# A hybrid state-space and delta-rule layer: the delta rule's inverse and decays on GpSimd, and two scalings of the state space as one GpSimd instruction for four heads

## The chip, the cores and the metric

The kernel runs on one core of a Trainium2 chip. The metric is the device time of one execution in microseconds (us), the median of several runs. The engines are TensorE (PE, with PEld for its weight loads), VectorE (DVE), ScalarE (ACT), GpSimd (POOL) and SyncE (SP), which issues nearly all DMAs. Each engine works through its own list of instructions in order; the lists meet only through semaphores.

## The reference

One layer over 1024 latent tokens and 256 context tokens of width 2048. The input is normed and modulated, multiplied by w_in, and the product is split; a short convolution follows, then two mixers side by side, a norm, and the product with w_out. The two places of the change lie in the mixers:

```
# delta rule (gdn_scan): 8 heads, 2 directions, chunks of 128 tokens
decay = exp(where(incl, gcum[:, None] - gcum[None, :], -inf))
a_strict = where(strict, (k_beta @ k.T) * decay, 0)
sol = triangular_solve(a_strict, rhs, unit_diagonal=True)
S = S * dec + ke.T @ v_new                  # scan over 10 chunks

# state space (ssd_scan): 16 heads in quarters of 4, 2 directions
lmat = exp(where(causal, seg, -inf))        # seg: differences of cumulated decays
states = B.T @ (x * dt * decay_end)
h = h * dec + states                        # scan over 10 chunks
```

## The kernel before, in words

The program is written as steps: blocks of 128 columns of the input projection ("g" for the delta rule, "s" for the state space, "z" for the gate), and for each head h of the delta rule "P" (prep), "I" (invert), "C" (chain) and "E" (end). A static scheduler of the kernel's framework orders the instructions of each engine when the program is built, and puts work of several steps between one another. So, while the chain of head h runs, TensorE also does the prep of head h+1 and products of the next blocks (line 437, 48 matmuls to a group, called *fill* below), and DVE the inverse of head h+1.

**Prep** (gdn_prep) goes over 10 chunks. A tile gb (four buffers) is loaded with the cumulated decays of both directions; `decay` (line 676) subtracts the column's own value and takes the minimum with a causal mask; ACT takes exp (690); DVE multiplies it with TensorE's k-by-k product into A (697), and with the k-by-q product (700), which is stored.

**invert_blocks** follows at once. DVE transposes the 32-wide diagonal blocks of A (715), they go to DRAM and come back as a tile X of 80 partitions, one block in each (721). Then 30 steps, each of two dependent instructions (726, 728), invert all of them: step k works on (31-k) rows of k numbers. X goes to DRAM (730) and comes back as xc (732).

**I** (invert) makes the full inverse from it: DVE transposes xc (741), ACT copies the blocks into A (746, 747), DVE fills the tile et (750 to 753), and TensorE's small products (770 to 794) do the rest. The last of them (794) ends the step. **C** (gdn_chain) is a scan of 10 steps for each of two directions; a step goes TensorE 850 and 852, DVE 856 (r), TensorE 866, DVE 871 and ACT 873 (x), TensorE 876 and 888, DVE 881 (the new state S) and 889 (the output o, from step 2 on). Each step loads its operand vq by an SP DMA (813). `finish_pair` (829 to 835) scales finished outputs, with five short GpSimd instructions to a pair.

**The state space** (ssd_quarter) runs four quarters of four heads. In `state`, ACT scales x by a column for each of four heads (941); GpSimd multiplies the old state (949). For the decays, a tile E is loaded, ACT adds a bias for each head and direction (989, eight instructions to a chunk), DVE selects and ACT takes exp.

In what follows C0 to C7 are the stretches in which the chains of heads 0 to 7 run; each ends with the last product (794) of the next head's I.

Of the kernel before, what the change touches and what calls it, by code (L numbers as in the profile page):

```python
# [14 lines left out]
P = 128  # L15
# [29 lines left out]
class Layer:  # L45
# [627 lines left out]
    def decay(self, e, d, h, c):  # L673

        nc = self.nc
        nc.vector.scalar_tensor_tensor(out=e, in0=e, scalar=self.G[:, 32 + d * 8 + h, c:c + 1],  # L676
                                       in1=self.mneg[:, d], op0=ALU.subtract, op1=ALU.min)

    def gdn_prep(self, h, D):
        nc, sp = self.nc, self.gp  # L680
# [24 lines left out]
    def invert_blocks(self, A):  # L705

        nc, sp = self.nc, self.gp
        t_ = lambda shape, name, **kw: sp.tile(shape, F32, tag=name, name=name, **kw)
        Q = 2 * NCH
        ft = t_([P, NCH, 32], "ft")  # L710
        d1 = self.dram.tile([Q, 4, 32, 32], F32, tag="d1", name="d1", bufs=2)
        d2 = self.dram.tile([Q, 4, 32, 32], F32, tag="d2", name="d2", bufs=2)
        for b in range(4):
            s = slice(32 * b, 32 * b + 32)
            nc.vector.transpose(out=ft[s], in_=A[s, 0, :, s])
            nc.sync.dma_start(out=d1[NCH:, b].rearrange("q j i -> j q i"), in_=A[s, 1, :, s])
        nc.sync.dma_start(out=d1[0:NCH].rearrange("q b j i -> (b j) q i"), in_=ft)

        X = t_([P, NCH * P], "X")[0:4 * Q, 0:1024].rearrange("p (a b) -> p a b", b=32)
        tp = t_([4 * Q, 256], "tp")  # L720
        nc.sync.dma_start(out=X, in_=d1.rearrange("q b j i -> (q b) j i"))
        for k in range(1, 31):
            m = 31 - k
            t = tp[:, 0:m * k].rearrange("p (a b) -> p a b", b=k)
            sh = [4 * Q, m, k]
            nc.vector.tensor_tensor(out=t, in0=X[:, k + 1:, k:k + 1].to_broadcast(sh),  # L726
                                    in1=X[:, k:k + 1, 0:k].to_broadcast(sh), op=ALU.mult)
            nc.vector.tensor_tensor(out=X[:, k + 1:, 0:k], in0=X[:, k + 1:, 0:k], in1=t, op=ALU.add)  # L728
        nc.gpsimd.memset(X.rearrange("p a b -> p (a b)")[:, ::33], 1.0)
        nc.sync.dma_start(out=d2.rearrange("q b j i -> (q b) j i"), in_=X)  # L730
        xc = t_([P, Q, 32], "xc")
        nc.sync.dma_start(out=xc, in_=d2.rearrange("q b j i -> (b j) q i"))
        return xc
# [181 lines left out]
    def ssd_quarter(self, Q, xT, BT, CT):  # L915
        nc, sp = self.nc, self.sp
        t_ = lambda shape, name, **kw: sp.tile(shape, F32, tag=name, name=name, **kw)
        R, PD = 4, 64
        hs = [slice(d * 16 + Q * R, d * 16 + Q * R + R) for d in range(2)]
        bc = lambda ap, n: ap.unsqueeze(2).to_broadcast([P, R, n])  # L920
        if Q % 2 == 0:
            self.btok = t_([P, NCH, P], "btok")
            for g, n in ((0, 4), (4, 4), (8, 2)):
                pt = self.ps("y")
                for i in range(n):
                    self.transpose(pt[:, i * P:(i + 1) * P], BT[:, (g + i) * P:(g + i + 1) * P])
                nc.scalar.copy(out=self.btok[:, g:g + n].rearrange("p c k -> p (c k)"), in_=pt[:, 0:n * P])
        btok = self.btok
        h4 = lambda ap: ap.rearrange("p (r q) -> p r q", q=PD)
        xs = t_([P, NCH, R, PD], "xs", bufs=2)  # L930

        def xtok(c):
            px = self.ps("x")
            for b in range(2):
                self.transpose(px[:, b * P:(b + 1) * P], xT[b][:, c * P:(c + 1) * P])
            nc.scalar.copy(out=xs[:, c], in_=h4(px[:, 0:2 * P]))

        def state(d, c, H, first):
            xd = t_([P, R, PD], "xd", bufs=3)
            for r in range(R):  # L940
                nc.scalar.activation(out=xd[:, r], in_=xs[:, c, r], func=AF.Copy, scale=self.dtw[:, hs[d].start + r, c:c + 1])
            pst = self.ps("h")[:, 0:R * PD]
            nc.tensor.matmul(out=pst, lhsT=btok[:, c], rhs=xd.rearrange("p r q -> p (r q)"),  # L943
                             start=True, stop=True)
            Hn = t_([P, R, PD], f"H{d}", bufs=2)
            if first:
                nc.scalar.copy(out=Hn, in_=h4(pst))
            else:
                nc.gpsimd.tensor_tensor(out=Hn, in0=H, in1=bc(self.cd[:, hs[d], c], PD), op=ALU.mult)
                nc.vector.tensor_tensor(out=Hn, in0=h4(pst), in1=Hn, op=ALU.add)  # L950
            return Hn

        def before(d, c, H):


            y = t_([P, 2, P], f"y{d}", bufs=3)
            for j in range(2):
                nc.sync.dma_start(out=y[64 * j:64 * j + 64],
                                  in_=self.er[hs[d], c * P:(c + 1) * P].rearrange("(b j) t -> j b t", j=2)[j].partition_broadcast(64))
            po = self.ps("z")[:, 0:R * PD]  # L960
            for b in range(2):
                nc.tensor.matmul(out=po[:, b * P:(b + 1) * P], lhsT=H[:, 2 * b:2 * b + 2].rearrange("p r q -> p (r q)"),  # L962
                                 rhs=CT[:, c * P:(c + 1) * P], start=True, stop=True)
            nc.vector.tensor_tensor(out=y, in0=po.rearrange("p (b t) -> p b t", t=P), in1=y, op=ALU.mult)
            return y

        H = None
        for i, c in enumerate([9, 8, 7, 6, 5, 4, 3, 2, 1, 0]):
            xtok(c)
            if c < NLC:  # L970
                y = before(1, c, H)
                for b in range(2):
                    xo = xT[b][:, c * P:(c + 1) * P]
                    nc.vector.scalar_tensor_tensor(out=xo, in0=xo, scalar=self.ssd_d[:, 2 * Q + b:2 * Q + b + 1],  # L974
                                                   in1=y[:, b], op0=ALU.mult, op1=ALU.add)
            if i < NCH - 1:
                H = state(1, c, H, i == 0)
        H = None
        for i, c in enumerate([8, 9, 0, 1, 2, 3, 4, 5, 6, 7]):
            s = slice(c * P, (c + 1) * P)  # L980
            if c < NLC:
                E = t_([P, 2, R, P], "E", bufs=2)
                for d in range(2):
                    nc.sync.dma_start(out=E[:, d], in_=self.gr[hs[d], s].partition_broadcast(P))

                for d in range(2):
                    for r in range(R):
                        j = d * 16 + Q * R + r
                        nc.scalar.activation(out=E[:, d, r], in_=E[:, d, r], func=AF.Identity, bias=self.G[:, j, c:c + 1])  # L989
                nc.vector.copy_predicated(out=E[:, 0], mask=self.mask[:, 1].bitcast(I32).unsqueeze(1).to_broadcast([P, R, P]), data=E[:, 1])  # L990
                nc.scalar.activation(out=E[:, 0], in_=E[:, 0], func=AF.Exp)
                nc.vector.copy_predicated(out=E[:, 0], mask=self.ident.bitcast(I32).unsqueeze(1).to_broadcast([P, R, P]),
                                          data=bc(self.dts[:, Q * R:Q * R + R, c], P))
                pc = self.ps("x")[:, 0:P]
                nc.tensor.matmul(out=pc, lhsT=BT[:, s], rhs=CT[:, s], start=True, stop=True)
                nc.vector.tensor_tensor(out=E[:, 0], in0=E[:, 0], in1=pc.unsqueeze(1).to_broadcast([P, R, P]), op=ALU.mult)
                y = before(0, c, H)
                for b in range(2):
                    nc.gpsimd.tensor_tensor(out=xT[b][:, s], in0=y[:, b], in1=xT[b][:, s], op=ALU.add)
                py = self.ps("y")  # L1000
                for r in range(R):
                    o = r % 2 * PD
                    nc.tensor.matmul(out=py[o:o + PD, r // 2 * P:r // 2 * P + P], lhsT=xs[:, c, r], rhs=E[:, 0, r],  # L1003
                                     start=True, stop=True)
                for b in range(2):
                    nc.vector.tensor_tensor(out=xT[b][:, s], in0=py[:, b * P:(b + 1) * P], in1=xT[b][:, s], op=ALU.add)
            if i < NCH - 1:
                H = state(0, c, H, i == 0)
        for b in range(2 if Q < 2 else 0):
            nc.sync.dma_start(out=self.yr[2 * Q + b], in_=xT[b][:, 0:NL])  # L1010
# [309 lines left out]
```

## Time and profile before

| | us |
|---|---|
| median of 3 runs (lowest, highest) | 2357.67 (2355.03, 2359.08) |
| the profiled execution's own time | 2351.73 |
| its span, first to last instruction | 2350.0 |
| TensorE busy | 2162.5 |
| DVE busy | 1399.5 |
| ACT busy | 998.5 |
| GpSimd busy | 268.7 |

Busy times come from one profiled execution. A TensorE that is shown as busy isn't at its peak: matmuls overlap, and the ends are modelled.

### The profile page before, as it was taken

The page shows a single profiled execution, that of the slowest core. Times are in us where ns is not written, and L with a number is a line of the kernel's source. Part 1 is how long each engine was busy: PE and PEld are TensorE (multiplying, and loading weights), DVE is VectorE, ACT ScalarE, POOL GpSimd, SP SyncE. Part 2 cuts the span into 40 slices and gives each one's busy share as a digit, 9 for nine tenths or more (in the row PEclk, how much of TensorE's full clock was granted, in tenths as well). Part 3 has the DMA queues.
Part 4 walks back from the last instruction along what each step waited for, and adds up shares of the span by engine and source line. Part 5 has one row for each costly group of instructions (what it writes and reads, how often), then busy time and mean ns, then how long its engine had stood idle before and what let it go on. Part 6 is the DMA issues. An engine that isn't in the chain of part 4 may idle for free. (4 is left out here: it accounts for less than half of the span.)

```text
span 2350.0 us, 41855 instructions
## 1 busy us (share of the span) xinstructions
PE 2162.5 (92%) x16070; PEld 1379.2 (59%) x16070; DVE 1399.5 (60%) x3499; ACT 998.5 (42%) x2493; POOL 268.7 (11%) x514
## 2 busy tenths in 40 slices
PE   4989999889999898998989999999999999899998
PEld 4334644456665655556555566555555555788887
DVE  5335543869694856858568486566767773511214
ACT  6026422344444352433524444465667584423320
POOL 1000001012111020111201110130303130000000
PEclk9999999999999999999999999999999999999999
DMA  9952347454444344343443444333465355212117
GB/s 323 348 164 55 80 145 217 117 131 106 134 115 120 101 126 116 88 133 93 121 119 85 127 123 115 99 90 108 111 183 149 98 164 195 68 37 73 55 37 269
DMA packets 397236, 301.71 MB, mean 128 GB/s; under 512 B 61339, under 2 KB 358684, under 8 KB 395628
## 3 DMA queue, kind: packets, MB, share of 16 engines
q1 hardware_dynamic: 386668, 293.80, 43.7%
q10 hardware_dynamic: 10368, 5.24, 0.8%
q8 instruction: 126, 2.06, 0.4%
q14 instruction: 74, 0.61, 0.1%
HBM read 241.41 MB, written 57.57 MB: 127 GB/s over the span
## 5 line engine op out<-in xcount | busy, mean ns | idle before, releaser
L437 PE MATMUL ps_d<-u,w 128*128 128x512 f16 (+1 forms) x4560 | 969.6, 357 | 8.3 <-DVE cv L498 4.6
L437 PEld LDWEIGHTS <-w 128*128 128x128 f16 x6048 | 595.3, 100 | 494.3 <-issue 36.4
L1138 PEld LDWEIGHTS <-u 128*128 128x128 f16 x3072 | 298.7, 98 | 50.9 <-DMA u<-in_w_out_dram 13.2
L437 PE MATMUL ps_e<-u,w 128*128 128x512 f16 (+1 forms) x1296 | 314.5, 376 | 0.0
L498 DVE SCALAR_TENSOR_TENSOR cv<-ps_d,taps,cv 128x496 f32<-128x496 f32 (+3 forms) x300 | 194.8, 650 | 80.0 <-ACT cv L492 38.6
L413 DVE SCALAR_TENSOR_TENSOR w<-w,scl 128x512 f16<-128x512 f32 (+1 forms) x204 | 149.9, 777 | 50.8 <-ACT w L411 50.3
L408 ACT ACTIVATE w<-w 128x1024 f16<-128x1024 f32 (+1 forms) x102 | 106.5, 1044 | 167.7 <-DMA w<-in_w_in_dram 101.5
L1138 PE MATMUL ps_d<-wx,u 128*128 128x256 f16 x1536 | 170.2, 273 | 4.6 <-DMA u<-in_w_out_dram 4.6
L1138 PE MATMUL ps_d<-w,u 128*128 128x256 f16 x1296 | 144.8, 273 | 5.7 <-DMA u<-in_w_out_dram 3.8
L1168 DVE SCALAR_TENSOR_TENSOR raw<-ps_d,inv,gp 128x256 f32<-128x256 f32 x59 | 28.4, 483 | 193.2 <-ACT jko L1166 193.2
L411 ACT ACTIVATE w<-w,scl 128x1024 f16<-128x1024 f32 (+1 forms) x102 | 112.3, 1133 | 36.2 <-DVE scl L145 16.5
L1166 ACT ACTIVATE jko<-ps_d,inv 128x256 f32<-128x256 f32 x59 | 27.8, 471 | 182.4 <-PE ps_d L1138 177.4
L989 ACT ACTIVATE E<-E,G 128x128 f32<-128x128 f32 x256 | 80.9, 388 | 35.1 <-DMA E<-gr 29.6
L690 ACT ACTIVATE gb<-gb 128x256 f32<-128x256 f32 x80 | 32.2, 413 | 147.0 <-DVE gb L676 144.0
L502 ACT ACTIVATE t<-cv 128x512 f32<-128x512 f32 (+1 forms) x98 | 55.7, 570 | 90.0 <-DVE cv L498 75.4
L676 DVE SCALAR_TENSOR_TENSOR gb<-gb,G,mneg 128x128 f32<-128x128 f32 x160 | 50.8, 345 | 69.2 <-DMA gb<-gr 67.9
L873 ACT ACTIVATE r<-ps_c,nb 128x128 f32<-128x128 f32 x128 | 45.7, 364 | 107.0 <-DVE xw L871 97.2
L876 PE MATMUL ps_c<-xw,vq 128*128 128x128 f32 x288 | 61.8, 304 | 30.8 <-DVE xw L871 14.2
L726 DVE TENSOR_TENSOR tp<-X 80x30 f32<-80x30 f32 (+14 forms) x240 | 77.6, 323 | 13.9 <-DMA X<-d 13.2
L876 PEld LDWEIGHTS ps_c<-xw,vq 128*128 128x128 f32 x288 | 47.4, 196 | 58.9 <-ACT r L873 33.7
L503 DVE SCALAR_TENSOR_TENSOR cv<-t,cv 128x512 f32<-128x512 f32 (+1 forms) x98 | 60.5, 618 | 31.7 <-ACT t L502 31.3
L728 DVE TENSOR_TENSOR X<-X,tp 80x30 f32<-80x30 f32 (+14 forms) x240 | 78.4, 327 | 0.6
(329 smaller groups left out, 3250.4 us busy)
## 6 DMA issues: line engine op xcount, KB each, us to landing
w<-in_w_in_dram SPq DMA_DIRECT2D x102, 512.0 KB
x<-in_w_ada_dram SPq DMA_DIRECT2D x48, 1024.0 KB
vq<-vq SPq DMA_DIRECT2D x128, 256.0 KB
E<-gr SPq DMA_DIRECT2D x64, 256.0 KB
u<-in_w_out_dram SPq DMA_DIRECT2D x24, 512.0 KB
gb<-gr SPq DMA_DIRECT2D x80, 128.0 KB
x<-in_x_dram SPq DMA_DIRECT2D x8, 1024.0 KB
vq<-gb SPq DMA_DIRECT2D x64, 128.0 KB
```

Source lines behind the costliest of these rows:

```text
L408: nc.scalar.activation(out=w16[h][:, 0], in_=w[h], func=AF.Square, accum_out=ssq[:, h:h + 1])
L411: nc.scalar.activation(out=w16[h][:, 0], in_=w[h], func=AF.Copy, scale=t)
L413: nc.vector.scalar_tensor_tensor(out=w16[h][:, 1, s], in0=w[h][:, s], scalar=t, in1=w16[h][:, 0, s], op0=ALU.mult, op1=ALU.subtract)
L437: self.nc.tensor.matmul(out=ps, lhsT=w16[k // KH][:, a, k % KH], rhs=self.u16[b][k][:, lo:lo + n], start=(k == 0 and i == 0), stop=(k == K ...
L498: nc.vector.scalar_tensor_tensor(out=o3[:, :, lo_o:hi_o], in0=p3[:, :, lo_o + s:hi_o + s], scalar=taps[tap], in1=o3[:, :, lo_o:hi_o], op0= ...
L502: nc.scalar.activation(out=t[:, 0:n], in_=o, func=AF.Tanh)
L503: nc.vector.scalar_tensor_tensor(out=o, in0=t[:, 0:n], scalar=1.0, in1=o, op0=ALU.add, op1=ALU.mult)
L726: nc.vector.tensor_tensor(out=t, in0=X[:, k + 1:, k:k + 1].to_broadcast(sh), in1=X[:, k:k + 1, 0:k].to_broadcast(sh), op=ALU.mult)
L728: nc.vector.tensor_tensor(out=X[:, k + 1:, 0:k], in0=X[:, k + 1:, 0:k], in1=t, op=ALU.add)
L876: nc.tensor.matmul(out=pS, lhsT=vq[:, 1], rhs=xw, start=True, stop=True)
L989: nc.scalar.activation(out=E[:, d, r], in_=E[:, d, r], func=AF.Identity, bias=self.G[:, j, c:c + 1])
L1138: self.nc.tensor.matmul(out=ps, lhsT=self.y16(k, p, s), rhs=w16[k // 4][:, q, k % 4], start=(i == 0 and j == 0), stop=(i == KB - 1 and j = ...
```

## The change

The decay of the delta rule becomes two GpSimd instructions (a subtraction with a minimum, then a causal select) in place of one of DVE. The two instructions of each of the inverse's 30 steps go from DVE to GpSimd. In the state space, four ACT instructions that scale x become one GpSimd instruction over four heads, and eight ACT instructions that add the bias become two.

```
@@ decay
-        nc.vector.scalar_tensor_tensor(out=e, in0=e, scalar=self.G[:, 32 + d * 8 + h, c:c + 1],
-                                       in1=self.mneg[:, d], op0=ALU.subtract, op1=ALU.min)
+        nc.gpsimd.tensor_scalar(out=e, in0=e, scalar1=self.G[:, 32 + d * 8 + h, c:c + 1], scalar2=0.0,
+                                op0=ALU.subtract, op1=ALU.min)
+        s = 1 - 2 * d
+        nc.gpsimd.affine_select(out=e, in_=e, compare_op=ALU.is_ge, fill=NEG, base=0, pattern=[[s, P]], channel_multiplier=-s)
@@ invert_blocks
-            nc.vector.tensor_tensor(out=t, in0=X[:, k + 1:, k:k + 1].to_broadcast(sh),
+            nc.gpsimd.tensor_tensor(out=t, in0=X[:, k + 1:, k:k + 1].to_broadcast(sh),
                                     in1=X[:, k:k + 1, 0:k].to_broadcast(sh), op=ALU.mult)
-            nc.vector.tensor_tensor(out=X[:, k + 1:, 0:k], in0=X[:, k + 1:, 0:k], in1=t, op=ALU.add)
+            nc.gpsimd.tensor_tensor(out=X[:, k + 1:, 0:k], in0=X[:, k + 1:, 0:k], in1=t, op=ALU.add)
@@ ssd_quarter
-            for r in range(R):
-                nc.scalar.activation(out=xd[:, r], in_=xs[:, c, r], func=AF.Copy, scale=self.dtw[:, hs[d].start + r, c:c + 1])
+            nc.gpsimd.tensor_tensor(out=xd, in0=xs[:, c], in1=bc(self.dtw[:, hs[d], c], PD), op=ALU.mult)
...
-                    for r in range(R):
-                        j = d * 16 + Q * R + r
-                        nc.scalar.activation(out=E[:, d, r], in_=E[:, d, r], func=AF.Identity, bias=self.G[:, j, c:c + 1])
+                    nc.gpsimd.tensor_tensor(out=E[:, d], in0=E[:, d], in1=bc(self.G[:, hs[d], c], P), op=ALU.add)
```

The scheduler orders every engine's list anew. Line numbers of the changed kernel are two higher than before between the decay and the state space (L749 is what was L747). Three places of the lists matter, all at the end of a chain, here that of C3; the other steady heads (C2, C4, C5) have the same order there.

ACT, at the end of the chain. Before:

```order
L873 ACTIVATE r_9294<-ps_c_9287,nb 128x128
L873 ACTIVATE r_9306<-ps_c_9299,nb 128x128
L829 ACTIVATE jk,ss<-o 128x128 x2
L411 ACTIVATE w<-w,scl 128x1024 x2
L490 ACTIVATE cv<-ps_d,taps 128x512
L502 ACTIVATE t<-cv 128x512
L690 ACTIVATE gb<-gb 128x256
L408 ACTIVATE w,wsq<-w 128x1024
L747 COPY A<-xc 32x10x32
```

and in the changed kernel:

```order
L875 ACTIVATE r_9549<-ps_c_9542,nb 128x128
L749 COPY A<-xc 32x10x32 x2
L875 ACTIVATE r_9567<-ps_c_9560,nb 128x128
L749 COPY A<-xc 32x10x32 x2
L748 COPY A<-xt 32x10x32 x4
L831 ACTIVATE jk,ss<-o 128x128 x2
L875 ACTIVATE r_9594<-ps_c_9587,nb 128x128
L875 ACTIVATE r_9606<-ps_c_9599,nb 128x128
L490 ACTIVATE cv<-ps_d,taps 128x512
```

The copies that need the inverse of the next head (L747, now L749) stood behind the chain's last x (L873, now L875); now the first of them stands ahead of the last three.

DVE, around its transpose of the inverse. Before, the last output of the chain (L889) stands more than a dozen rows ahead of these:

```order
L676 SCALAR_TENSOR_TENSOR gb<-gb,G,mneg 128x128
L498 SCALAR_TENSOR_TENSOR cv<-ps_d,taps,cv 128x8x62
L498 SCALAR_TENSOR_TENSOR cv<-ps_e,taps,cv 128x254
L741 STREAM_TRANSPOSE xt<-xc 128x640
L503 SCALAR_TENSOR_TENSOR cv<-t,cv 128x512
```

and in the changed kernel:

```order
L873 TENSOR_SCALAR xw_9568<-ps_c_9560,pw 128x128
L413 SCALAR_TENSOR_TENSOR w<-w,scl 128x512
L891 TENSOR_TENSOR o<-ps_c_9542,o 128x128
L743 STREAM_TRANSPOSE xt<-xc 128x640
L883 SCALAR_TENSOR_TENSOR S_9572<-S_9527,cd,ps_c_9560 128x128
L858 SCALAR_TENSOR_TENSOR r_9590<-ps_c_9587,eG,vq_9556 128x128
L862 SCALAR_TENSOR_TENSOR o<-ps_c_9587,eG,o 128x128
L891 TENSOR_TENSOR o<-ps_c_9560,o 128x128
```

The transpose (L741, now L743) has moved ahead of the chain's last state (L883) and of all DVE work of its last step.

SP, the DMA queue. Before:

```order
L813 DMA vq_9256<-vq 128x512
L813 DMA vq_9274<-vq 128x512
L811 DMA vq_10496<-vq 128x256
L811 DMA vq_10498<-vq 128x256
L811 DMA vq_10508<-vq 128x256
L811 DMA vq_10518<-vq 128x256
L730 DMA d_8874<-X 80x1024
L394 DMA w<-in_w_in_dram 128x8x128
L732 DMA xc<-d_8874 128x20x32
```

and in the changed kernel:

```order
L815 DMA vq_9529<-vq 128x512
L732 DMA d_9174<-X 80x1024
L815 DMA vq_9556<-vq 128x512
L734 DMA xc<-d_9174 128x20x32
L815 DMA vq_9574<-vq 128x512
L394 DMA w<-in_w_in_dram 128x8x128
```

The write of the inverted blocks (L730, now L732) and the read of xc (L734) have moved ahead of the operands of the chain's last step (L813, now L815).

## Rows read from the trace of the kernel before

**Rows 1.** First line of the page.

```profile
span 2350.0 us, 41855 instructions
```

**Rows 2.** Busy time by stretch: C1 to C6, each to the end of I.

```profile
618.00:749.00 131.00, 124.57 (x986) 78.24 (x983) 96.27 (x281) 56.22 (x150) 20.14 (x40) 1.00 0.46 122
749.00:897.00 148.00, 135.64 (x1041) 84.81 (x1036) 101.09 (x289) 57.47 (x151) 20.76 (x40) 0.98 0.42 110
897.00:1041.00 144.00, 133.84 (x1016) 83.69 (x1016) 99.56 (x286) 57.53 (x151) 20.70 (x40) 0.98 0.44 112
1041.00:1188.00 147.00, 135.20 (x1017) 84.08 (x1016) 99.49 (x285) 57.54 (x151) 20.69 (x40) 0.97 0.43 110
1188.00:1337.00 149.00, 135.56 (x1018) 84.40 (x1017) 99.72 (x286) 57.52 (x151) 20.71 (x42) 0.97 0.42 108
1337.00:1435.00 98.00, 88.08 (x738) 56.11 (x738) 71.75 (x225) 34.59 (x83) 11.03 (x29) 0.97 0.46 124
```

The columns after the stretch are its length, then busy us (and instructions) of PE, PEld, DVE, ACT and POOL, the granted TensorE clock, the DMA share and GB/s.

**Rows 3.** The same view inside C3: the inverse, and the stretch behind the chain.

```profile
970.00:1030.00 60.00, 57.72 (x420) 30.69 (x418) 32.76 (x70) 35.40 (x94) 13.27 (x23) 1.00 0.46 120
936.00:970.00 34.00, 33.29 (x212) 23.32 (x213) 32.39 (x121) 10.91 (x33) 6.79 (x16) 1.00 0.27 74
```

**Rows 4.** Lines of C3: durations ns min/median/max, first and last start us.

```profile
L697 DVE SCALAR_TENSOR_TENSOR A<-gb,nb,ps_m x20: 340/342/348, 896.7 to 921.9; 128x128 f32<-128x128 f32 x20
L715 DVE STREAM_TRANSPOSE ft<-A x4: 493/502/508, 922.2 to 923.7; 32x320 f32<-32x320 f32 x4
L889 DVE TENSOR_TENSOR o<-ps_c,o x16: 278/286/292, 924.2 to 969.6; 128x128 f32<-128x128 f32 x16
L770 PE MATMUL ps_m<-xt,ft x40: 191/191/212, 1029.7 to 1030.7; 32*32 32x32 f32 x40
```

**Rows 5.** Tiles X and xc in C3, the same columns.

```profile
L726 DVE TENSOR_TENSOR tp<-X x30: 199/334/395, 936.2 to 969.3; 80x30 f32<-80x30 f32 x2, 80x58 f32<-80x58 f32 x2, 80x84 f32<-80x84 f32 x2, 80x108 f32<-80x108 f32 x2
L730 SPq DMA_DIRECT2D d<-X x1: 1642/1642/1642, 970.1 to 970.1; - x1
...
L747 ACT COPY A<-xc x4: 448/455/458, 979.8 to 987.4; 32x320 f32<-32x320 f32 x4
L732 SPq DMA_DIRECT2D xc<-d x1: 371/371/371, 974.1 to 974.1; - x1
```

**Rows 6.** The chain's output in C7, where no prep and no inverse run beside it.

```profile
L889 DVE TENSOR_TENSOR o<-ps_c,o x16: 278/292/293, 1443.3 to 1479.4; 128x128 f32<-128x128 f32 x16
```

**Rows 7.** GpSimd: one line's durations, then groups (count, busy us, mean ns).

```profile
L664 POOL TENSOR_TENSOR cv<-cv,kn x24: 606/1035/1504, 400.8 to 1310.9; 128x512 f32<-128x512 f32 x16, 128x256 f32<-128x256 f32 x8
...
L949 POOL TENSOR_TENSOR H<-H,cd 128x256 f32<-128x256 f32 x64 | 47.1, 736 | 114.9 <-ACT H L947 68.0 <-DVE H L950 46.7
L999 POOL TENSOR_TENSOR cv<-y,cv 128x128 f32<-128x128 f32 x64 | 32.2, 524 | 37.3 <-DVE y L964 33.9 <-DMA y<-er 3.5
L822 POOL TENSOR_SCALAR si<-inv 128x8 f32<-128x8 f32 x8 | 3.3, 416 | 0.7
L112 POOL TENSOR_SCALAR_AFFINE_SELECT mneg<-mneg 128x128 f32<-128x128 f32 x2 | 0.5, 292 | 0.0
```

**Rows 8.** GpSimd's timeline: start us, us, instruction.

```profile
953.62 0.20 POOL L831 TENSOR_TENSOR ss<-ss,s 128x2 f32<-128x2 f32 x1 [58.75 <-ACT jk L829]
953.91 0.24 POOL L832 TENSOR_SCALAR ss<-ss 128x2 f32<-128x2 f32 x1
...
955.42 0.70 POOL L835 TENSOR_TENSOR o<-o,ss 128x256 f32<-128x256 f32 x1
...
1011.55 1.45 POOL L664 TENSOR_TENSOR cv<-cv,kn 128x512 f32<-128x512 f32 x1
```

**Rows 9.** Groups that the change removes: busy us, mean ns, idle before.

```profile
L676 DVE SCALAR_TENSOR_TENSOR gb<-gb,G,mneg 128x128 f32<-128x128 f32 x160 | 50.8, 345 | 69.2 <-DMA gb<-gr 67.9 <-issue 1.2
L989 ACT ACTIVATE E<-E,G 128x128 f32<-128x128 f32 x256 | 80.9, 388 | 35.1 <-DMA E<-gr 29.6
L941 ACT ACTIVATE xd<-xs,dtw 128x64 f32<-128x64 f32 x288 | 75.5, 341 | 3.2 <-PE ps_h L943 2.8
```

**Rows 10.** The chain that ended last: start us, us, what.

```profile
1525.25 19.03 PE ps_d L437 x88
```

## The prediction

> **What bounds the kernel now.** I read the windows by head first, because the span [rows 1] does not say where time is lost. C2 to C5 are alike: 148, 144, 147 and 149 us [rows 2]. TensorE is shown as busy nine tenths of that, but this is no measure of its work, since matmuls stretch when they wait. A better one is the pace of an undisturbed stretch, 19.03 us for 88 matmuls of 512 columns, 0.216 us each [rows 10].
>
> Then I cut C3 (897 to 1041) into pieces by the first and last starts of four lines [rows 4]: prep from 896.7 to 921.9 (25 us, L697), the transposes of the blocks to about 924 (L715), the chain's outputs from 924.2 to 969.6 (L889), and I from 1029.7 (L770) on, 11 us. Between the chain's end and I lie 60 us of dense fill [rows 3]. The inverse runs inside the chain: X arrives at 936.2 (14 us behind prep), its write is issued at 970.1 (34 us later), and xc is in ACT's hands at 979.8 (9.7 us) [rows 5]. So inverse and chain end together, and I, which needs xc, starts 50 us later. Before, the inverse could be late at no cost.
>
> In those 34 us DVE is busy 32.4 [rows 3]: there DVE is the bound. Seven steps' outputs take 45.4 us in C3 [rows 4] and 36.1 in C7, which has no inverse beside it [rows 6]: 6.5 us a step against 5.2. What stands on DVE can thus be worth something; the question is what else moves.
>
> **The change, part by part.**
>
> *The inverse's price on GpSimd.* No row shows these shapes there. Step k handles (31-k)k numbers, 4960 over all steps: two instructions each, so 60 instructions and 9920 elements. GpSimd's two-input instructions take 0.20 us for 2 elements [rows 8], 0.606 at the least for 256 and 1.035 in the median of L664, which is mostly 512 [rows 7]. That is 0.20 us and about 1.64 ns an element. Dependent ones follow one another with 0.09 us between them (953.62 plus 0.20 to 953.91 [rows 8]); I take 0.08. The sum is 60 x 0.20 + 9920 x 1.64 ns + 60 x 0.08 = 12.0 + 16.3 + 4.8 = 33 us. Bounds: 28 without gaps; 45 if all were stretched as the L664 of 1.45 us is over the median (1.4 times 28.3, plus gaps) [rows 7, 8]. I take 33, since shapes of 30 to 240 elements lie between rows that I have. It is about what the inverse took on a shared DVE.
>
> The Trainium skill's GPSIMD Engine Reference (3.1, Elementwise) has 4497 ns for a two-input add of 2048 elements, near 2.2 ns an element, and calls VectorE about twice as fast. The rows here say 1.64; by the page's figure the estimate would be 39 us, and the kernel some 36 us slower than by mine.
>
> *What now waits for it.* This decides the case. The new lists put work that needs xc inside the chain: ACT's first copies stand ahead of the chain's last three x, DVE's transpose ahead of its last state, and SP's write and read ahead of the operands of its last step. Engines work in order, so the last one and a half steps of C2 to C5 can't run before xc has landed. C1 has two x behind the first copy, C6 one. TensorE's list holds most fill behind the chain, so TensorE waits too.
>
> *A steady head anew.* Decays on GpSimd: a chunk has two instructions for each direction, 0.42 (L822, a price for 8 elements) and 0.29 (L112) [rows 7], 1.4 us together against 0.69 on DVE (two of L676, 345 ns [rows 9]). Four buffers make three rounds of the ten chunks, each 0.7 later: 2 us. Bounds 0 (DVE no longer waits for gb, 67.9 us over all heads [rows 9], which can pay for it) and 7 (0.7 for each chunk). So prep is 27; then 14 to X, 33 for the inverse, 9.7 to xc, 5 for the rest of the chain (one step at the pace of C7): the chain ends 89 us into the head, where it took 73 (897 to 970), 16 later. The fill behind it grows from 263 matmuls to 295 by the new list: 32 x 0.216 = 7, so 67 us for 60. With 11 for I the head takes 167 against 144: 23 more, 92 in four heads.
>
> *The others.* C1: 16 for the same wait, 2.5 since a pair of finish_pair (five instructions, 953.62 to 956.12 [rows 8]) now stands among the inverse, 13 for 60 more matmuls, less 1 for a shorter rest: 30. C6: 16 + 2.5, less 2: 17 (the windows of both before are in [rows 2]). C0 has all its x ahead of the copies, so no such wait, but 83 more matmuls less what hides in gaps: 16; they come from the stretch ahead of the first I, which waits for the first inverse and gives nothing back. 41 matmuls move from C6 into the dense fill behind it: 9. In all 92 + 30 + 17 + 16 + 9 = 164.
>
> *What DVE is relieved of* (some 20 us of inverse in a head, 60 of 0.33 by L726's median [rows 5], and 7 of decays) I price at nothing: the chain ends with xc. Without that wait it is worth the first rival below.
>
> *The state space.* A chunk loses eight instructions of 388 ns [rows 9] for two of 1.035: 3.1 us become 2.1. The scaling loses four of 341 [rows 9] for one of 128x256, 0.74 by L949 [rows 7]: 1.36 become 0.74. All in series, a quarter (8 and 18 of them) would gain 8 + 11 = 19 us, 76 in four. Against that: ACT waited 29.6 us for E to load [rows 9], which stays, and now holds up GpSimd's list with the states in it; and the new list has some 46 matmuls (10 us) fewer inside a quarter's chain, to be done behind it. I take nothing, with 76 as the bound of a gain and 40 (four times 10) of a loss.
>
> *Sum.* 2351.7 (the profiled execution, 1.7 above its span) + 164 = 2516; the median of the runs shown lies 6 above that execution, so 2522.
>
> **The rivals.**
>
> *GpSimd is quick enough (ends faster).* If an instruction of the inverse took 0.2 us, it would be done in 12, and xc would land 61 us into a head, when the chain is about to end by itself. The chain would go at TensorE's pace (31 us of matmuls behind prep, 33 with gaps), and quick decays add nothing: 25 + 2 + 33 + 67 + 11 = 138, 6 less than now, 24 in four heads. C1 comes out even (13 less, 13 more), C6 gains 13, C0 and the fill behind C6 still cost 25, and the first inverse, which all waits for, gives 22: 34 less in all, 2324. It turns at those 12 us. For it: the lists are set as if it were so. Against: 0.20 is the row of 2 elements, and the mean here is 165. Chance 4%.
>
> *GpSimd is slower than in quiet rows.* If short rows of elements or DVE's instructions hold the inverse up as they hold that L664, it takes 45 us, 12 more in six heads: 72, so 2594. For it: L999 and L949 have means of 524 and 736 ns [rows 7], where 0.20 plus 1.64 ns an element gives 410 and 620. Against: while the chain waits for xc, DVE has little to do. The Trainium skill's page SBUF — State Buffer (Who interferes with whom) says that a GpSimd instruction that reads SBUF and a VectorE one with two SBUF inputs lock one another out; the row of 1.45 us agrees in size, and most of the chain's DVE instructions take an input from PSUM. Chance 20%.
>
> *The state space pays back.* All 76 us are gained: 2446. Chance 12%.
>
> *The wait is covered.* Were fill that I count behind the chain to run during the wait, the four heads would stay near 144 and the rest near even: no change. The list has no such fill but in C0. Chance 2%.
>
> **How the numbers follow.** The forecast as summed has 62%: 2522, its own range 2465 to 2570 (inverse 28 to 38, prep 0 to 7, half the state space's bounds). The range reaches from the third rival's side to just beyond the second, 2430 to 2605. About 0.2% (5 us) is what a measurement of this kernel can tell from no change. Faster 5% (the first rival, with a little over), within that 2%, slower 93%.
>
> **What the profile would show.** Right: from X's arrival to its write 30 to 38 us on GpSimd; in C2 to C5 ACT's first copy and DVE's transpose wait for the DMA of xc, 15 us and more each; TensorE is idle there, with a lower granted clock; these heads take some 167 us, 67 of them between the last output and I. Wrong: the copies wait for nothing (first rival); the 60 instructions take over 0.7 us in the mean (second); the quarters after 1546 shrink by 15 us or more each (third). The forecast falls if xc lands before the chain's last step, since all but 25 us of the sum hang on that wait.

## The result, and the profile after

The changed kernel takes 2640.43 us (median of 4 runs, 2633.14 to 2641.99) against 2358.38 us before, run beside it on the same chip: a ratio of 1.1189 [1.1161, 1.1217], 282 us slower. The direction was forecast; the size was not: 164 us were forecast, and the time lies 35 us above the range. TensorE's mean granted clock fell from 0.978 to 0.932 of full speed.

First the first line of the page (before: [rows 1]) and the windows of C0 to C3 and C6, each to the end of I, and of the rest (columns as in [rows 2], where C1 to C6 of before stand; C4 and C5 are like C3):

```profile
span 2639.2 us, 41796 instructions
...
506.00:670.00 164.00, 143.77 (x1048) 88.74 (x1046) 85.30 (x212) 63.43 (x192) 76.62 (x148) 0.93 0.39 105
670.00:835.00 165.00, 134.00 (x996) 83.78 (x993) 80.41 (x202) 56.21 (x150) 68.49 (x140) 0.90 0.36 97
835.00:1010.00 175.00, 140.75 (x1031) 86.72 (x1027) 83.11 (x205) 57.23 (x151) 69.48 (x140) 0.90 0.35 93
1010.00:1186.00 176.00, 139.34 (x1021) 85.70 (x1019) 83.11 (x206) 57.14 (x151) 69.49 (x140) 0.90 0.35 92
...
1536.00:1651.00 115.00, 83.35 (x709) 53.95 (x704) 51.97 (x147) 33.06 (x81) 51.55 (x111) 0.88 0.39 107
1651.00:2639.00 988.00, 896.29 (x6177) 618.49 (x6173) 496.60 (x1002) 301.57 (x588) 221.19 (x319) 0.97 0.35 107
```

Set against before, by the ends of I (read to 1 or 2 us), this is where the 289 us of the two spans went:

| stretch | before | after | more | forecast |
|---|---|---|---|---|
| to the end of the first I | 494 | 506 | 12 | 0 |
| C0 | 124 | 164 | 40 | 16 |
| C1 | 131 | 165 | 34 | 30 |
| C2 to C5 | 588 | 701 | 113 | 92 |
| C6 | 98 | 115 | 17 | 17 |
| behind C6 (C7, state space, output) | 915 | 988 | 73 | 9 |

Then C3 (1010 to 1186) by the tiles X and xc, as in [rows 5]:

```profile
L728 POOL TENSOR_TENSOR tp<-X x30: 234/516/1052, 1058.6 to 1094.5; 80x30 f32<-80x30 f32 x2, 80x58 f32<-80x58 f32 x2, 80x84 f32<-80x84 f32 x2, 80x108 f32<-80x108 f32 x2
...
L749 ACT COPY A<-xc x4: 453/455/458, 1102.0 to 1103.8; 32x320 f32<-32x320 f32 x4
...
who waited for it (us, times):
  ACT A L749: 21.1, 1
  DVE xt L743: 18.7, 1
```

X arrives 49 us into the head, the inverse lasts 36 (1058.6 to 1095), xc is there at 1102, and ACT and DVE have waited 21.1 and 18.7 us for it. ACT's timeline shows what stands behind the waiting copy: the chain's x of L875, on which TensorE's next step rests.

```profile
1080.56 0.37 ACT L875 ACTIVATE r<-ps_c,nb 128x128 f32<-128x128 f32 x1 [0.23 <-DVE xw L873]
1102.03 0.93 ACT L749 COPY A<-xc 32x320 f32<-32x320 f32 x2 [21.10 <-DMA xc<-d]
1102.98 0.37 ACT L875 ACTIVATE r<-ps_c,nb 128x128 f32<-128x128 f32 x1
```

Over the whole span, the waits (engine, line, what it waited for; us in total, times, longest):

```profile
ACT gb L692 <- POOL gb L679: 220.8, 73, 13.3
...
ACT A L749 <- DMA xc<-d: 144.9, 7, 24.1
PE ps_c L878 <- ACT r L875: 135.7, 26, 20.1
POOL gb L676 <- DMA gb<-gr: 131.4, 27, 12.1
```

And the new instructions on GpSimd by shape (busy us, mean ns, idle before), which answer to the groups of [rows 9] and the estimates from [rows 7]:

```profile
L676 POOL TENSOR_SCALAR gb<-gb,G 128x128 f32<-128x128 f32 x160 | 114.6, 727 | 191.5 <-DMA gb<-gr 131.4 <-DVE r L858 12.4 <-DVE S L883 11.9
L988 POOL TENSOR_TENSOR E<-E,G 128x512 f32<-128x512 f32 x64 | 71.5, 1122 | 69.6 <-DMA E<-gr 64.2 <-PE ps_x L994 4.3 <-DMA y<-er 0.6
L942 POOL TENSOR_TENSOR xd<-xs,dtw 128x256 f32<-128x256 f32 x72 | 49.1, 685 | 93.2 <-ACT xs L938 79.3 <-PE ps_h L944 13.9
...
L679 POOL TENSOR_SCALAR_AFFINE_SELECT gb<-gb 128x128 f32<-128x128 f32 x160 | 44.0, 297 | 0.0
```

### The profile page after: what moved, and what is told of

Read it like the earlier page. It is cut to its first block, busy times and chain, and to the rows that moved or that the text cites. A ratio compares the mean times of both kernels' runs of the same rounds, so it can differ in the third digit from the quotient of the medians.

```text
span 2639.2 us, 41796 instructions
## 1 busy us (share of the span) xinstructions
PE 2232.5 (85%) x16070; PEld 1411.8 (53%) x16070; DVE 1275.4 (48%) x2859; ACT 853.7 (32%) x1949; POOL 778.2 (29%) x1450
## 4 chain that ended last, share of the span: by engine, by line
PE 41%; POOL 15%; DMA 12%; DVE 6%; issue 5%; ACT 4%; SPq 1%; POOLq 0%; DVEq 0%; ACTq 0%
PE ps_d L437 18%; PE ps_d L1137 11%; PE ps_e L437 6%; POOL X L730 5%; POOL tp L728 5%; DMA gb<-gr 3%; DMA E<-gr 2%; DMA vq<-gb 1%; DMA u<-in_w_out_dram 1%; POOL E L988 1%; DMA xc<-d 1%; DVE cv L498 1%; POOL gb L676 1%; DMA d<-X 1%; PE ps_c L878 1%
## 5 line engine op out<-in xcount | busy, mean ns | idle before, releaser
L437 PE MATMUL ps_d<-u,w 128*128 128x512 f16 (+1 forms) x4560 | 984.8, 362 | 8.2 <-DVE cv L498 5.3
L437 PEld LDWEIGHTS <-w 128*128 128x128 f16 x6048 | 602.8, 101 | 515.3 <-issue 57.2
L437 PE MATMUL ps_e<-u,w 128*128 128x512 f16 (+1 forms) x1296 | 325.4, 385 | 2.0 <-DVE cv L498 1.9
L498 DVE SCALAR_TENSOR_TENSOR cv<-ps_d,taps,cv 128x496 f32<-128x496 f32 (+3 forms) x300 | 195.8, 653 | 120.1 <-ACT cv L490 67.7
L676 POOL TENSOR_SCALAR gb<-gb,G 128x128 f32<-128x128 f32 x160 | 114.6, 727 | 191.5 <-DMA gb<-gr 131.4
L408 ACT ACTIVATE w<-w 128x1024 f16<-128x1024 f32 (+1 forms) x102 | 106.5, 1045 | 160.9 <-DMA w<-in_w_in_dram 93.4
L1137 PE MATMUL ps_d<-w,u 128*128 128x256 f16 x1296 | 144.9, 273 | 5.8 <-DMA u<-in_w_out_dram 3.6
L730 POOL TENSOR_TENSOR X<-X,tp 80x30 f32<-80x30 f32 (+14 forms) x240 | 129.5, 540 | 17.1
L728 POOL TENSOR_TENSOR tp<-X 80x30 f32<-80x30 f32 (+14 forms) x240 | 121.8, 508 | 40.9 <-DMA X<-d 23.9
L483 POOL TENSOR_SCALAR taps<-cw_gdn,inv 128x5 f32<-128x5 f32 x24 | 8.6, 358 | 340.7 <-DVE inv L160 318.1
L502 ACT ACTIVATE t<-cv 128x512 f32<-128x512 f32 (+1 forms) x98 | 55.8, 571 | 132.3 <-DVE cv L498 103.9
L699 DVE SCALAR_TENSOR_TENSOR A<-gb,nb,ps_m 128x128 f32<-128x128 f32 x160 | 48.9, 344 | 91.9 <-ACT gb L692 82.3
L988 POOL TENSOR_TENSOR E<-E,G 128x512 f32<-128x512 f32 x64 | 71.5, 1122 | 69.6 <-DMA E<-gr 64.2
```

The costliest lines, as they stand in the source:

```text
L408: nc.scalar.activation(out=w16[h][:, 0], in_=w[h], func=AF.Square, accum_out=ssq[:, h:h + 1])
L437: self.nc.tensor.matmul(out=ps, lhsT=w16[k // KH][:, a, k % KH], rhs=self.u16[b][k][:, lo:lo + n], start=(k == 0 and i == 0), stop=(k == K ...
L498: nc.vector.scalar_tensor_tensor(out=o3[:, :, lo_o:hi_o], in0=p3[:, :, lo_o + s:hi_o + s], scalar=taps[tap], in1=o3[:, :, lo_o:hi_o], op0= ...
L502: nc.scalar.activation(out=t[:, 0:n], in_=o, func=AF.Tanh)
L676: nc.gpsimd.tensor_scalar(out=e, in0=e, scalar1=self.G[:, 32 + d * 8 + h, c:c + 1], scalar2=0.0, op0=ALU.subtract, op1=ALU.min)
L728: nc.gpsimd.tensor_tensor(out=t, in0=X[:, k + 1:, k:k + 1].to_broadcast(sh), in1=X[:, k:k + 1, 0:k].to_broadcast(sh), op=ALU.mult)
```

## The experiments

The theory: the largest part of the loss is not that GpSimd is slow, but that in the lists of ACT, DVE and SP the work that needs xc stands ahead of the chain's last steps. Rivals: GpSimd's own time and traffic; the decays; the state space. Medians and ratios are against the kernel before, run on the same chip in the same rounds; its median was 2359.7 to 2361.7 us.

### One part at a time: e1_inverse, e2_decays, e3_state_space

Each has one hunk of the change and the rest as before: e1 the two lines of the inverse, e2 the function decay, e3 the two hunks of the state space.

> Only the inverse's 60 instructions a head go to GpSimd. Theory (the lists): in the changed kernel ACT's first copies of xc waited 145 us for the DMA of xc in seven heads, since they stand ahead of the chain's last x; the inverse itself takes 36 us there against 34 before. So this part alone brings that wait: some 20 us in each of six heads, 120 to 150 us slower in all. Rival (the decays): the later prep (X arrives 49 us after the end of I, where it was 40 before) makes the lateness, and the inverse alone costs under 60 us.

> Only the decays go to GpSimd, the inverse stays on DVE. ACT's copies of xc stand behind the chain's last x here. Theory (the lists): prep ends some 8 us later in a head (GpSimd's subtraction takes 727 ns in the changed kernel), but the inverse's result has 50 us to spare: 10 to 50 us slower. Rival (the decays): most of the delta rule's 220 us, so over 100 us slower.

> Only the two edits of the state space. In the changed kernel the stretch behind the delta rule took 988 us against 915, 73 more, of which some 17 are matmuls moved there from heads. Theory: the loss is the state space's own, a quarter's chain grew from 65 to 76 us: 45 to 70 us slower. Rival: it comes from the delta rule's delay (matmuls moved, a lower clock), and this part alone is within 15 us of before, or faster.

Measured: e1 2543.37 us, 1.0768 [1.0744, 1.0793], 182 more; e2 2422.34 us, 1.0255 [1.022, 1.029], 61 more; e3 2411.20 us, 1.0201 [1.0174, 1.0229], 50 more. They sum to 293 for the 282 of the whole, so the parts hardly help or hinder one another. All three cost more than the prediction gave them: some 150 for the inverse, some 12 for the decays (2 us in each of six heads), nothing for the state space. e1 and e2 also cost more than these theories allowed (150 and 50); e3 lies inside its range, and none of the three rivals occurred. In C3 of e1 the first copy of xc runs 86 us into the head, where it ran at 84 before: the inverse is hardly later, and yet the head takes 167 us for 144.

### The order alone: e4_inverse_behind_chain, e5_inverse_behind_fill

e4 is e1 with the work that needs xc queued behind the chain on each engine: the copies behind its last x, the transpose behind its last o, the DMAs of the inverse behind its last load.

```
-                self.invert(heads[m]["T"], heads[m]["xc"])
+                with ExitStack() as after:
+                    for i in (heads[m]["last"] or ())[0:2]:
+                        after.enter_context(self.tc.issue_after(i))
+                    self.invert(heads[m]["T"], heads[m]["xc"])
```

> As e1, with the order of three lists changed and nothing else: SP writes and reads the inverse behind the chain's last operand load, and ACT's copies and DVE's transpose of xc stand behind the chain's last x and last output. Theory (the lists): the wait inside the chain is gone, so the loss of e1 goes with it: within 30 us of the kernel before, on either side (DVE has 20 us less to do in a head, I may begin later). Rival (GpSimd's rate, or its contention with DVE): the loss of e1 stays within 20 us.

Measured: 2471.66 us, 1.0472 [1.0445, 1.0499], 110 more: neither the theory's 30 nor the rival's 162 and above. The chain was free (its outputs end 68 us into a head, 73 before), yet heads took 156. The timeline of ACT in C3 says why:

```profile
1027.34 0.19 ACT L839 ACTIVATION_READ_ACCUMULATOR jk<-o 128x1 f32 x1
1042.93 1.86 ACT L757 COPY A<-xc 32x320 f32<-32x320 f32 x4 [15.41 <-DMA xc<-d]
...
1046.68 0.63 ACT L502 ACTIVATE t<-cv 128x512 f32<-128x512 f32 x1
1047.22 0.67 ACT L490 ACTIVATE cv<-ps_d,taps 128x512 f32<-128x512 f32 x1
```

The same wait, one place further down: the copies now hold up ACT's evictions of the convolution (L502, L490) and, behind them, the split of the next weights (L408); on DVE the transpose, which waited 14.8 us, holds up that engine's share of the evictions (L498). TensorE waits for both engines in turn (3.7 us for DVE's eviction of its bank ps_d, 4.9 for L408) and starts 8 matmuls between 1043 and 1053. So e5 puts the copies and the transpose behind the last eviction (i on ACT, j on DVE) of the head's second convolution block, close to where the kernel before has them:

```
+            self.ev[col] = i.ins, j.ins
...
-                    for i in (heads[m]["last"] or ())[0:2]:
+                    late = self.ev[OFF_QKV + (17 + m) * P if m < 7 else 2 * P] if m else ()
+                    for i in (heads[m]["last"] or ())[0:2] + late:
```

> Inverse on GpSimd as in e4, and in addition the eight copies on ScalarE and the transpose on VectorE that need xc are queued behind the last eviction of the second convolution block of the same head (in C6 behind the chain's last x, as in e4). In e4 these two engines stood still for 15 us behind the chain, in front of evictions for which TensorE's fill waits. Theory (the loss is the place in the in-order lists of what needs xc, not GpSimd's speed: xc lands 85 us into a head in e1 and e4 and 86 before): C1 to C5 come to 142 to 150 us, the kernel to 2365 to 2410 us; what is left is C0, C6 and the stretch behind C6. Rival (the inverse on GpSimd costs by itself: its other work, such as the finishing of output pairs and the scaling of taps, is late behind it, and it hinders VectorE): heads stay at 152 to 157 us and the kernel at 2440 us or above.

Measured: 2390.76 us, 1.0140 [1.0101, 1.0180], 31 more: as the theory expected, but for C1 and C5, which at 132 and 141 us came out below its 142 to 150. With the same 60 instructions on the same engine, order alone took back 151 of 182 us. C2, C3, C6 and the rest in e5:

```profile
779.00:922.00 143.00, 134.70 (x1016) 82.67 (x1014) 88.04 (x225) 56.73 (x151) 53.23 (x100) 0.98 0.43 113
922.00:1065.00 143.00, 133.64 (x1018) 82.20 (x1018) 88.74 (x227) 56.84 (x151) 52.27 (x100) 0.99 0.43 113
...
1348.00:1459.00 111.00, 83.78 (x699) 52.61 (x698) 54.72 (x161) 32.93 (x81) 41.09 (x89) 0.86 0.40 109
1459.00:2389.00 930.00, 877.79 (x6167) 610.02 (x6166) 484.23 (x1000) 443.39 (x1132) 101.81 (x183) 0.99 0.38 114
```

C2 to C5 take 143, 143, 142 and 141 us, 1 to 8 less than in [rows 2], though xc comes no earlier (it is transposed 84 to 87 us into a head in both): in C3 DVE has 11 us less to do, and the chain's outputs end at 67 in place of 73. What is lost lies at the ends: C6 111 against 98, since no convolution block is left to put the copies behind and the wait of 19.5 us stays; the stretch behind it 930 against 915; C0 144 against 124; 9 us ahead of the first I.

### No inverse at all: e6_inverse_left_out

```
-        for k in range(1, 31):
...
-            nc.vector.tensor_tensor(out=X[:, k + 1:, 0:k], in0=X[:, k + 1:, 0:k], in1=t, op=ALU.add)
+        nc.gpsimd.memset(X, 0.0)
```

> The kernel before without the 60 instructions of the inverse; X is filled with zeros by one GpSimd instruction instead, so the inverse of the blocks is not computed and the output is another. Its lists are made anew and put what needs xc inside the chain too, as far as the order was set for an early xc, but xc now really is early (some 50 us into a head). Theory (a list that expects xc early costs only when xc is late): no wait for xc, the chain's outputs end 65 to 70 us into a head, heads of 138 to 147 us, the kernel at 2290 to 2355 us. Rival (the new lists lose by themselves, by fewer matmuls beside the chain and more behind it): heads of 150 us or more, the kernel above 2390 us.

The run leaves out the 60 instructions and fills X with zeros. Measured: 2357.81 us, 0.9996 [0.9983, 1.0009]. Neither theory nor rival: the lists don't lose by themselves, nor is anything won. The first I ends 30 us earlier, C6 is 8 shorter, C2 to C5 up to 6 each; C0 pays 30 (1101 matmuls for 949 before) and the stretch behind C6 23. TensorE has the same work to do, and what leaves one stretch comes back in another. So with lists made by the scheduler alone the inverse on VectorE cost this kernel nothing, and there was nothing for another engine to win.

### A version that is faster: e9_five_heads_behind_fill, and its control e12_order_without_gpsimd

e5 won inside C1 to C5 and lost at the ends. e9 keeps the five heads and gives the others back to VectorE; e12 has the order of e9 with all inverses on VectorE.

```
-        D["xc"] = self.invert_blocks(A)
+        D["xc"] = self.invert_blocks(A, self.nc.gpsimd if 2 <= h <= 6 else self.nc.vector)
```

> As e5 for the inverses of heads 2 to 6 alone, which run beside C1 to C5; those of heads 0, 1 and 7 stay on VectorE with the order of before. In e5, C1 to C5 took 17 us less than before, while the first inverse, C0, C6 and the stretch behind C6 took 48 more. Theory (VectorE's relief is worth some 4 us a head where nothing waits for xc): C1 to C5 keep the 17 us and the rest returns to before, so 2335 to 2352 us. Rival (the gain is only fill that moves between stretches, as leaving the inverse out altogether gave nothing): 2355 us or more.

> The order of e9 with every inverse on VectorE: the control for e9. Theory (e9's gain is VectorE's relief, 20 us of work a head taken from beside the chain): C1 to C5 as before, 2355 to 2370 us. Rival (the order by itself gains, whichever engine inverts): 2350 us or less.

Measured: e9 2342.40 us, 0.9913 [0.9898, 0.9929], 19 us faster than before; e12 2358.64 us, 0.9993 [0.9974, 1.0011]. Both as the theory expected: the order alone gives nothing, GpSimd alone loses, the two together gain. C3, C4 and C6 of e9:

```profile
895.00:1037.00 142.00, 134.68 (x1016) 83.06 (x1015) 88.19 (x226) 56.76 (x151) 52.16 (x100) 0.98 0.45 114
1037.00:1180.00 143.00, 132.01 (x1017) 81.34 (x1016) 88.71 (x226) 56.87 (x151) 52.55 (x100) 1.00 0.42 113
...
1322.00:1421.00 99.00, 87.80 (x737) 56.03 (x736) 71.70 (x225) 34.61 (x83) 10.99 (x29) 0.97 0.48 123
```

GpSimd is busy 52 us in a head for 21 before, and C1 to C5 together take 700 us for 719; ahead of the first I and behind C6 the profiled execution loses some 10 of these again.

### The decays: e11_one_direction_of_decays

```
     def decay(self, e, d, h, c):
+        if d == 0:
+            nc.vector.scalar_tensor_tensor(out=e, in0=e, scalar=self.G[:, 32 + d * 8 + h, c:c + 1],
+                                           in1=self.mneg[:, d], op0=ALU.subtract, op1=ALU.min)
+            return
```

> Only the decays, and of these only direction 1 on GpSimd, direction 0 on VectorE as before. Theory (the two directions' 2.05 us a chunk on GpSimd set the pace at which the blocks are prepared, and at 1.02 us they no longer do): 2360 to 2380 us, X arriving at most 2 us later in a head than before. Rival (the price is the hand from GpSimd to ScalarE, whose queue holds the chain's x behind it, whatever GpSimd's share): 2400 us or more.

Measured: 2373.01 us, 1.0046 [1.0029, 1.0064], 11 more against 61 with both directions: the time is as the theory expected. X comes 42 to 44 us behind the last product of I in C2 to C5 (41 to 42 before, 46 to 48 in e2), 2 to 4 us later than before, where the theory allowed 2. That GpSimd's busy time sets the pace is not shown: in the first 29 us of C3 in e2 it is busy 12 and waits for loads of gb most of the rest. ACT, whose list has the exponentials of gb among the chain's x, waits for GpSimd. Waits of e2 over the span (ACT's wait for the decay was 144.0 us before, then on DVE, and TensorE's for x 13.4):

```profile
ACT gb L692 <- POOL gb L679: 215.3, 71, 13.5
POOL gb L676 <- DMA gb<-gr: 152.6, 28, 12.6
...
PE ps_c L878 <- ACT r L875: 46.7, 21, 4.9
```

So both ends of the delta rule slip: X by 6 us, and the chain's last outputs, which end 81 to 84 us into C2 to C5 for 73 to 76. How much of the 50 us between e2 and e11 is GpSimd's duration and how much the place of the exponentials in ACT's list was not separated.

### The state space: e7_scaling_alone, e8_biases_alone

Each has one of the two hunks.

> Of the change only the scaling of x in the state space: one GpSimd instruction for four heads in place of four on ScalarE. Theory (the loss of e3 is the biases on GpSimd, which stand in its list ahead of the states' own steps and wait for their loads): 2350 to 2378 us, the state chain of a quarter lasting 37 to 43 us as before. Rival (the scaling carries it, since scaling and decay of the state now follow one another on one engine in every one of 18 steps): 2385 us or more.

> Of the change only the biases of the decays in the state space: one GpSimd instruction for four heads in place of four on ScalarE. Theory: the most of e3's 50 us, so 2388 to 2412 us, with the decay of the state on GpSimd waiting behind a bias that waits for its load. Rival (the scaling carries the loss): 2350 to 2375 us.

Measured: e7 2378.60 us, 1.0087 [1.0058, 1.0115], 19 more; e8 2384.54 us, 1.0123 [1.0087, 1.0160], 25 more. The theory that the biases carry nearly all falls: the two share the loss. The steps of the state (first to last start of L943, L942 in e7 and e3, L944 after) last 37 to 44 us in a quarter before, 41 to 45 in e7, 41 to 48 in e8, and with both hunks 50 to 54, in e3 as in the changed kernel: 43 us more over the four quarters. The first quarter before and after:

```profile
L943 PE MATMUL ps_h<-xd,btok x36: 379/379/483, 1547.7 to 1585.1; 128*128 128x256 f32 x36
...
L944 PE MATMUL ps_h<-xd,btok x36: 378/382/635, 1781.0 to 1832.3; 128*128 128x256 f32 x36
```

In e8 ACT waits where it did not (waits of e8 over the span):

```profile
ACT E L989 <- DVE E L988: 89.7, 26, 10.1
POOL E L987 <- DMA E<-gr: 48.4, 30, 5.2
DVE E L988 <- POOL E L987: 38.8, 23, 4.2
```

Before, ACT added the biases itself, waited 29.6 us for the loads [rows 9] and 6.6 for DVE. Now a load releases GpSimd, GpSimd DVE, and DVE ACT's exponential, behind which ACT's other work stands. GpSimd's timeline in the same kernel shows the other side, the decay of the state (L949) between biases that wait for loads:

```profile
1700.08 0.62 POOL L949 TENSOR_TENSOR H<-H,cd 128x256 f32<-128x256 f32 x1
1701.74 1.05 POOL L987 TENSOR_TENSOR E<-E,G 128x512 f32<-128x512 f32 x1 [1.03 <-DMA E<-gr]
...
1704.03 1.04 POOL L987 TENSOR_TENSOR E<-E,G 128x512 f32<-128x512 f32 x1
1705.04 0.62 POOL L949 TENSOR_TENSOR H<-H,cd 128x256 f32<-128x256 f32 x1
```

### The whole change in e5's order: e10_whole_behind_fill

> The whole change with the order of e5. Theory (the wait in the lists is its largest part, and the rest adds up: 31 of e5, 61 of the decays, 50 of the state space): 2470 to 2515 us. Rival (late decays bring xc some 10 us later into a head than in e5, past the place to which its users were put, and the wait comes back): 2550 us or more.

Measured: 2520.26 us, 1.0668 [1.0645, 1.0691]: 120 us less than the whole change, 5 above what the theory allowed and far from the rival. The parts here add up to 142 and cost 159 together. Nothing waits for xc in C3, but the chain's outputs end 78 us into a head for 67 in e5, and the head takes 155. Late decays alone put these outputs some 8 us later (e2), so most of it is likely theirs; a run that shows it was not made.

## Why the prediction was right and wrong

By the table, the two spans differ by 125 us more than was forecast: 64 behind C6, 36 in C0 and ahead of it, 21 in C2 to C5, 4 in C1. The wait that the forecast hung on was right; the steps that failed are the state space, priced at nothing, the decays, priced at 2 us a head, and what the new lists do ahead of the first I and in C0.

**What bounds, and the main step: right.** The forecast hung on one wait: ACT's copies, DVE's transpose and SP's DMAs that need xc stand inside the chain. The trace shows it where it was put (21.1 and 18.7 us in C3, 144.9 on ACT over all), and e5 shows that it is the cause: moved, the same instructions cost 31 us in place of 182.

**The inverse's price: slightly low.** 33 us forecast, 36.4 measured (1058.6 to 1095.1 in C3). By the figure of the Trainium skill's GPSIMD Engine Reference (3.1, Elementwise), near 2.2 ns an element, the estimate was 39; the measurement lies between the two. The rival that GpSimd is slower than in quiet rows (45 us) is refuted, though its 2594 us lie nearer to the result.

**The decays' price: the step that failed in the heads.** I took 0.42 us for a decay's first instruction from L822, a row of 8 elements, and 2 us for the preparation, with bounds of 0 to 7. L676 takes 727 ns in the mean, and e2 alone costs 61 us. One chunk in C3 of the changed kernel:

```profile
1022.69 1.40 POOL L676 TENSOR_SCALAR gb<-gb,G 128x128 f32<-128x128 f32 x2 [0.78 <-DMA gb<-gr]
1024.05 0.54 POOL L679 TENSOR_SCALAR_AFFINE_SELECT gb<-gb 128x128 f32<-128x128 f32 x2
```

That is 1.94 us for the 1.4 I had. In C3, X came 49 us into the head where 41 was forecast (43, counted like the 49 from the last product itself): 6 to 8 of the 9 us by which the head missed its 167. My three rounds of buffers would make 4 us of the 1.94, 2 more than forecast, so the rounds were too few as well; how a round lengthens was not traced. The rest of it is close: 36.4 for 33, 6.9 for 9.7 to xc, 8.9 for 5 to the chain's end, 65 for 67 of fill, 10 for 11 of I.

**C0 and the first inverse: mis-sized, 52 us for 16.** I said that C0 has no such wait, since all its x stand ahead of the copies. Its x do not wait, but the copies do, behind the last x, as in e4:

```profile
591.03 0.36 ACT L875 ACTIVATE r<-ps_c,nb 128x128 f32<-128x128 f32 x1
605.79 0.94 ACT L749 COPY A<-xc 32x320 f32<-32x320 f32 x2 [14.40 <-DMA xc<-d]
```

TensorE then waits 4.6 us for the split of the next weights (L408). The chain ended 14 us later (86 us into the head for 72), and 10 of these stand at its start: its first product with A starts 12 us into C0, and 2 before. This comes with the inverse and not with the decays: it starts at 12 in e1, e4 and e5 too, and at 1 in e2. The first inverse, for which all wait, came 8 us later and lasted 38 us for 32; I had given this stretch nothing.

**The state space at nothing: the step that failed behind C6.** 73 us for 9; in e3, with the state space alone, this stretch takes 973 us for 915. I took durations in series, 8 times 388 ns and 4 times 341; ACT's short instructions overlap. Two rows of the timeline of ACT before:

```profile
1666.62 1.06 ACT L941 ACTIVATE xd<-xs,dtw 128x64 f32<-128x64 f32 x4
...
1692.06 2.14 ACT L989 ACTIVATE E<-E,G 128x128 f32<-128x128 f32 x7
```

Four scalings took 1.06 us, not 1.36; seven biases 2.14, not 2.7, so that eight take 2.4, hardly more than GpSimd's two of 1.12. Of the 76 us of gain some 33 were there (8 times 0.2 and 18 times 0.37 in each of four quarters), and the bound of a loss, 40, was made of moved matmuls alone. I had named the wait for loads in GpSimd's list and put no price on it, and had not seen the hand over three engines; the steps of the state grew by 43 us, and what each of the two gives of it was not separated. The rival that the state space pays back is refuted by e3. The rest of the 73 us comes with the inverse: the stretch behind C6 takes 15 us more in e5, 23 in e6 and 27 in e1, where I counted 9 for the 41 matmuls (x6167 for x6126) that move there. What else is late in it was not traced.

**VectorE's relief at nothing: right here, wrong as a rule.** e6 shows that taking the inverse away wins nothing in the lists as made; e9 shows 19 us once the order lets the chain end early.

**The other rivals.** GpSimd quick enough, and the wait covered by fill: neither occurred, and both were given little.

## What to carry to other kernels

When work moves to a slower engine, ask first where the in-order lists put what needs its result: here an order written out by hand turned 182 us of loss into 31, and for five heads of eight into a gain of 19. Time short instructions by the distance between their starts and price an operation by a row of its own shape; the row of 8 elements was worth 0.42 us and the real one 0.73. Before an engine is relieved, leave the work out altogether once: that the time stayed at 2358 us said in one run that relief was worth nothing in the order that the scheduler makes.

## What the runs showed of the hardware

- On GpSimd, the two instructions of an inverse step took 240 and 253 ns for 30 numbers and 628 and 688 for 240 (means over eight heads of the changed kernel), so some 0.19 us and 1.9 to 2.1 ns a number; on VectorE before, 200 and 189, and 396 and 395, so 0.17 us and some 0.95 ns. I had 1.64 ns from larger shapes.
- A TENSOR_SCALAR of 128x128 on GpSimd with a scalar for each partition took 727 ns in the mean, 0.70 in quiet stretches, longer than the two-input addition of 128x128 there (L998, 557 ns). I had priced it at 0.42.
- TensorE's granted clock falls in the stall. Windows of C3 after the change (columns as above, the granted clock third from the end):

```profile
1080.00:1096.00 16.00, 3.38 (x19) 1.68 (x18) 3.31 (x9) 0.70 (x4) 13.94 (x30) 0.70 0.01 3
1096.00:1101.00 5.00, 0.00 (x0) 0.00 (x0) 0.00 (x0) 0.00 (x0) 3.36 (x9) 0.50 0.86 181
1101.00:1106.00 5.00, 2.60 (x9) 1.96 (x10) 1.68 (x4) 3.85 (x9) 0.00 (x0) 0.50 0.99 280
1106.00:1111.00 5.00, 4.70 (x26) 3.16 (x25) 2.59 (x10) 2.00 (x8) 1.94 (x5) 0.92 0.20 55
1111.00:1116.00 5.00, 5.00 (x25) 2.25 (x23) 3.77 (x6) 1.49 (x6) 2.61 (x8) 1.00 0.10 30
```

  It is at 0.50, the level of 1.2 GHz, behind a stretch of 16 us with 3.4 of matmuls, and at 1.00 again in the stretch that begins 8 us after the first matmul of the restart (1103.4). With so few matmuls in those stretches it adds little to the wait itself.
